# Seven half-block products for the second MLP matrix of a one-core hybrid decoder block, with weight sums added by GpSimd's transfers

## The chip, the cores and the metric

The kernel runs on one core of a Trainium2 chip. The metric is device time in microseconds (us), the median of three runs. TensorE (PE) multiplies, VectorE (DVE) and ScalarE (ACT) do elementwise work, GpSimd (POOL) does little here, and SyncE (SP) issues nearly all transfers. In the profile "PEld" is TensorE's loading of the stationary operand.

## The reference

One layer on a sequence of 512 tokens with 1024 channels: an RMS norm, a token mixer of three branches (mLSTM, GLA, gated DeltaNet), a residual sum, and an MLP with a last norm. What the change mainly touches is the MLP:

```python
u = rmsnorm(x, g_norm_mlp[l])                       # x: (1, 512, 1024)
x = x + jnp.square(jax.nn.relu(u @ w_mlp_in[l])) @ w_mlp_out[l]   # 1024 -> 4096 -> 1024
return rmsnorm(x, g_final)
```

## The kernel before, in words

All large products are made of three float32r matmuls (`mm3`): each operand is split into a rounded part "h" and the rest "l", and l·h, h·l and h·h are added in PSUM. Splitting an operand takes a copy to the rounded type (on ScalarE or VectorE, `either`) and a subtraction on VectorE. Weights come as 512 KB transfers of 128 partitions with 1024 columns into a pool "raw" of three buffers, and are split into pools "wh" and "wl" of three buffers each (`load_w`). `load_w1` does the same for 512 columns in general slots; there are 44 slots of 128x512.

No instruction is placed by hand. `write_block` records all operations in a graph; `Graph.schedule` puts the matmul groups in the order that `plan` names and places every other operation by a list scheduler with fixed costs per operation and due times. `emit` then writes the instructions in that order, so each engine's queue is a fixed sequence and an instruction that waits holds up all behind it. The constant `EVAC` sets how long after its matmuls a PSUM evacuation is due; a transfer is planned at 190e3 bytes per us.

**The first step** ("mv"): for each of eight blocks of 128 channels, SP loads a block of the transposed x (`xk`) and of a weight (`mv0r`, ...). ScalarE scales x by the norm's gain, which lies in `pr`; GpSimd's queue loads `pr`. TensorE makes 96 matmuls into four PSUM banks. Ten warming products of ones come first. For the norm, `gen_u` squares each block (ScalarE), adds the squares (VectorE), and TensorE sums them over the partitions (`token_sums`).

**Before the MLP**, `gen_x2` does the same sum for the second norm, and transposes the residual x2 to token-major tiles. The norm's factor is only needed per token, because relu squared is homogeneous: `r2c` scales the result of the second MLP matrix.

**The MLP** has eight groups of 512 hidden channels. `mlp_in(g)` makes four chunks of 128 channels (24 matmuls of 512 columns each), then relu, square and split into `ah`, `al`. `mlp_out(g)` multiplies with 512 rows of the second matrix: 2 halves of the columns x 4 token tiles x 4 blocks of rows x 3 = 96 matmuls, and VectorE adds each of the eight results, scaled by `r2c`, to x2. The order is mi0, mi1, mo0, mi2, mo1, ... mo7. In the last group each x2 tile is squared after its sum (`square_of`), and `finish` computes the norm's factor and writes a token tile out; the last tile's last half is done in two pieces of 256 columns.

PSUM has eight banks: class "g" (four) holds matmul groups, class "m" (four) the transposes and small products.

The lines that the steps name: `plan`, `gen_u`, `token_sums`, `load_w1`, `gen_x2`, `mlp_in`, `mlp_out`, `square_of`, `finish`, and in the graph `due`, `run` and `record`. All engine work is issued from line 525.

Of the kernel before, what the change touches and what calls it, by code (L numbers as in the profile page):

```python
# [23 lines left out]
NWARM = 10  # L24
# [22 lines left out]
EVAC = 5.0  # L47
# [62 lines left out]
class Op:  # L110
    __slots__ = ("i", "eng", "calls", "cost", "lat", "preds", "succs", "tiles", "main", "fset", "kind", "start", "fin", "lst", "npred", "ready", "new", "tag", "nbytes", "evac", "alts")


class Graph:
    def __init__(self, nc):
        self.nc = nc
        self.ops = []
        self.main_key = None
        self.open = None
        self.shadow = __import__("concourse.bacc", fromlist=["Bacc"]).Bacc("TRN2", target_bir_lowering=False, num_devices=1)  # L120
        self.ntile = 0
# [34 lines left out]
    def record(self, eng, method, a, k):  # L156
# [18 lines left out]
        self.gate = []  # L175
# [99 lines left out]
    def due(self, pin, end):  # L275
# [45 lines left out]
    def run(self, mains, caps, horizon, verbose=False):  # L321
# [66 lines left out]
        while done < total:  # L388
# [147 lines left out]
def plan():  # L536

    seq = """mv mo dk0 mq1 sc mk0 dq1 dq0 mk1 mq0 dk1 gt01 dv0 gt00 dv1 gt02 lq0 gt03 gt20 up00 up02 lk0 lq1 lv lk1 up03 dz up01
    gt22 gt13 up20 gt12 gt21 up21 lr gt23 up22 up23 gt10 up10 up12 gt11 up11 up13 wo mi0""".split()
    for g in range(1, 8):  # L540
        seq += [f"mi{g}", f"mo{g - 1}"]
# [22 lines left out]
def write_block(nc, xT, w_cm, w_tm, w_sc, w_up, w_out, w_mi, w_mo, w_lr, prm, cst, g_fin, out):  # L564
# [58 lines left out]
    nc.gpsimd.dma_start(pr, prm)  # L623
    nc.gpsimd.dma_start(cs[:, :C_LV], cst[:, :C_LV])
# [13 lines left out]
    def token_sums(pss, sums):  # L638
        for t in range(4):
            mm(pss[:, t:t + 1], sums[:, blk(t)], ones)  # L640

    pss = mps("pss")
    rc = one("rc", [P, 4])


    for i in range(NWARM):
        mm(pss[:, P:2 * P], onem, onem)

    def gen_u():
# [8 lines left out]
        nc.vector.tensor_scalar(v, pss[:, :4], 1.0 / D, EPS, op0=ALU.mult, op1=ALU.add)  # L658
# [29 lines left out]
    def load_w1(src, name):  # L688
# [4 lines left out]
        nc.either.copy(h_, r)  # L693
# [72 lines left out]
    pmv = [gps(f"mvp{t}") for t in range(4)]  # L766
    for k in range(8):
# [9 lines left out]
        wh, wl = load_w1(w_tm[G_MV, k // 2, :, k % 2], f"mv{k}")  # L777
        for t in range(4):
            mm3(pmv[t], h_[:, blk(t)], l_[:, blk(t)], wh, wl, k == 0, k == 7)
# [11 lines left out]
    nc.scalar.dma_start(cs[:, C_LV:], cst[:, C_LV:])  # L791
# [14 lines left out]
    eall = one("em", [P, 4, 4, 2, P])  # L806
# [527 lines left out]
    def lv_evac(t, ps):  # L1334
        lv[t] = slot(f"lv{t}")
# [22 lines left out]
    pss2 = mps("pss2")  # L1358
    r2c = one("r2c", [P, 4])

    def gen_x2():
        acc = slot("x2acc")
        for d in range(8):
            sq = tmp(f"x2sq{d}") if d else acc
            nc.scalar.activation(sq, x2T[d], AF.Square)
            if d:
                nc.vector.tensor_add(acc, acc, sq)
            if d == 7:
                token_sums(pss2, acc)
# [30 lines left out]
    gf = [None, None]  # L1400

    def mlp_in(g):
        hs_ = []
        stage[0] = f"mi{g}"
        for i in range(4):
            wh, wl = load_w(w_mi[g * 4 + i], f"mi{g}{i}")
# [5 lines left out]
            a_h = slot("ah", F32R)  # L1412
            a_l = slot("al", F32R)
            nc.scalar.activation(a_h, rl, AF.Square)
            nc.vector.tensor_mul(rl, rl, rl)
            nc.vector.tensor_sub(a_l, rl, a_h.bitcast(F32))
            hs_.append((a_h, a_l))
        return hs_

    def mlp_out(g, hs_):  # L1420
        last = g == NG - 1
        stage[0] = f"mo{g}"
        wts = []
        for hf in range(2):
            w_ = []
            for i in range(2):
                if last and hf:
                    w_ += [load_w1(w_mo[g, hf, i, :, kk], f"mo{g}{hf}{i}{kk}") for kk in range(2)]
                else:
                    wh, wl = load_w(w_mo[g, hf, i], f"mo{g}{hf}{i}")  # L1430
                    w_ += [(wh[:, kk], wl[:, kk]) for kk in range(2)]
            wts.append(w_)
        if last:

            for hf, t, c0, n in [(hf, t, 0, 512) for hf in range(2) for t in range(3)] + [(0, 3, 0, 512), (1, 3, 0, 256), (1, 3, 256, 256)]:
                cl = slice(c0, c0 + n)
                ps = gps(f"mop{g}{t}{hf}{c0}")[:, :n]
                for k in range(4):
                    mm3(ps, hs_[k][0][:, blk(t)], hs_[k][1][:, blk(t)], wts[hf][k][0][:, cl], wts[hf][k][1][:, cl], k == 0, k == 3)
                o = x2[t][hf][:, cl]  # L1440
                nc.vector.scalar_tensor_tensor(o, ps, r2c[:, t:t + 1], o, op0=ALU.mult, op1=ALU.add)
                square_of(t, o)
                if hf and c0 + n == 512:
                    finish(t)
            return
        for hf in range(2):
            for t in range(4):
                ps = gps(f"mop{g}{t}{hf}")
                for k in range(4):
                    mm3(ps, hs_[k][0][:, blk(t)], hs_[k][1][:, blk(t)], wts[hf][k][0], wts[hf][k][1], k == 0, k == 3)  # L1450
                nc.vector.scalar_tensor_tensor(x2[t][hf], ps, r2c[:, t:t + 1], x2[t][hf], op0=ALU.mult, op1=ALU.add)
# [4 lines left out]
    def square_of(t, o):  # L1456
# [3 lines left out]
        if nsq[t] == 1:  # L1460
            nc.vector.tensor_mul(o, o, gf[0])

    def finish(t):

        nc.vector.tensor_mul(x2[t][1], x2[t][1], gf[1])
        f = fss[:, 3 * t:3 * t + 3]
        v, s, y, h = (small(f"f{n}", 1) for n in "vsyh")
        nc.vector.tensor_scalar(v, f[:, 0:1], f[:, 1:2], D * EPS, op0=ALU.add, op1=ALU.add)
        if nsq[t] == 3:
            nc.vector.tensor_add(v, v, f[:, 2:3])  # L1470
        nc.scalar.activation(s, v, AF.Sqrt)
        nc.vector.reciprocal(y, s)

        nc.vector.tensor_scalar(h, y, y, v, op0=ALU.mult, op1=ALU.mult)
        nc.vector.tensor_scalar(h, h, -0.5, 1.5, op0=ALU.mult, op1=ALU.add)
        for hf in range(2):
            nc.vector.tensor_scalar(x2[t][hf], x2[t][hf], y, h, op0=ALU.mult, op1=ALU.mult)
            (nc.scalar if hf else nc.sync).dma_start(out[blk(t), blk(hf, 512)], x2[t][hf])

    prev = mlp_in(0)  # L1480
    for g in range(1, NG):
        cur = mlp_in(g)
        if g == NG - 1:
            gf = [slot(f"gf{hf}") for hf in range(2)]
            for hf in range(2):
                nc.sync.dma_start(gf[hf], g_fin[blk(hf, 512)].partition_broadcast(P))
                nc.vector.tensor_scalar_mul(gf[hf], gf[hf], float(D) ** 0.5)
# [28 lines left out]
def _layout(inp):  # L1516
# [18 lines left out]
    for r in (4, 36, 68):  # L1535
# [14 lines left out]
             w_lr=w_lr, prm=p, cst=_consts(), g_fin=f('g_final'))  # L1550
# [19 lines left out]
```

## Time and profile before

| | |
|---|---|
| median of 3 runs | 976.89 us (976.88 to 976.90) |
| profiled execution | 976.91 us, its span 975.1 us |
| mean granted TensorE clock | 0.996 |
| PE / PEld / DVE / ACT / POOL busy | 99% / 82% / 60% / 42% / 1% of the span |
| moved by transfers | 94.64 MB, mean 97 GB/s |

The span runs from the first to the last instruction; the execution's own time is 1.8 us longer. Busy times are shares of the span; an engine with idle time costs nothing unless the engine that sets the end waits for it.

### The profile page before, as it was taken

Reading aid. Unit: us, or ns where it says so; the run is one execution under the profiler, and the core shown is the slowest. Engines: PE = TensorE matmul, PEld = TensorE weight load, DVE = VectorE, ACT = ScalarE, POOL = GpSimd, SP = SyncE. Lnnn points to the kernel's source line nnn. Section 1 sums busy time; section 2 is a strip of 40 time slices with the busy share of each in tenths; the row PEclk is TensorE's granted clock in tenths of the full one; section 3 lists DMA queues with packets and bytes.
Section 4 is the critical chain, followed back from the end, with each engine's and each line's share of the span. In section 5 each row is a group of like instructions: output and inputs, shape, how many; then the busy total and the mean of one; then the engine's idle time right before and its main releaser. Section 6 shows DMA issues by size and latency. Waiting matters only on the chain.

```text
span 975.1 us, 12773 instructions
## 1 busy us (share of the span) xinstructions
PE 964.2 (99%) x4992; PEld 804.0 (82%) x4992; DVE 580.9 (60%) x1065; ACT 408.5 (42%) x764; POOL 5.4 (1%) x20
## 2 busy tenths in 40 slices
PE   8999999999999999999999999999999999999996
PEld 7888888888888888888888888888888888888885
DVE  6667867778525765777647665444454445544446
ACT  6454466533523664544244434442423233232313
POOL 0000000000000000000000000000000000000000
PEclk9999999999999999999999999999999999999998
DMA  7222532222411222212224222222323224322302
GB/s 269 87 87 87 170 113 95 57 87 88 123 58 66 75 98 87 88 66 76 75 89 142 96 90 94 86 98 87 108 87 109 88 84 153 128 87 87 108 22 87
DMA packets 37028, 94.64 MB, mean 97 GB/s; under 512 B 7804, under 2 KB 11900, under 8 KB 36968
## 3 DMA queue, kind: packets, MB, share of 16 engines
q1 hardware_dynamic: 36152, 92.51, 29.5%
q10 hardware_dynamic: 720, 1.08, 0.3%
q8 instruction: 39, 0.64, 0.3%
q0 software_dynamic: 96, 0.24, 0.1%
q14 instruction: 21, 0.17, 0.1%
HBM read 91.17 MB, written 2.65 MB: 96 GB/s over the span
## 4 chain that ended last, share of the span: by engine, by line
PE 98%; DVE 0%; DMA 0%; ACT 0%; issue 0%; DVEq 0%; POOLq 0%
PE mop L525 20%; PE mip L525 18%; PE upp L525 7%; PE wop L525 4%; PE mvp L525 2%; PE lrp L525 2%; PE dzp L525 2%; PE lvp L525 2%; PE ll L525 2%; PE gt22p L525 1%; PE gt13p L525 1%; PE gt20p L525 1%; PE gt12p L525 1%; PE gt21p L525 1%; PE dq0p L525 1%; PE dv0p L525 1%
## 5 line engine op out<-in xcount | busy, mean ns | idle before, releaser
L525 DVE SCALAR_TENSOR_TENSOR x<-mop,r2c,x 128x512 f32<-128x512 f32 (+1 forms) x65 | 48.1, 741 | 54.0 <-PE mop L525 53.9
L525 DVE TENSOR_TENSOR lw<-lbs 128x260 f32<-128x260 f32 (+12 forms) x52 | 21.0, 448 | 7.9 <-PE ll L525 7.8
L525 DVE SCALAR_TENSOR_TENSOR sg<-sg,upp 128x512 f32<-128x512 f32 x24 | 16.4, 685 | 15.5 <-PE upp L525 15.4
L525 ACT ACTIVATE lw<-lw 128x512 f32<-128x512 f32 x28 | 17.4, 630 | 14.1 <-DVE lw L525 13.8
L525 DVE TENSOR_TENSOR al<-rl,ah 128x512 fp32r<-128x512 f32 x32 | 22.0, 689 | 0.8
L525 DVE TENSOR_TENSOR rl<-rl 128x512 f32<-128x512 f32 x32 | 22.1, 692 | 0.0
L525 PEld LDWEIGHTS ll<-lwq,lw 128*17 128x17 f32 (+3 forms) x320 | 17.5, 131 | 4.3 <-issue 1.4
L525 ACT ACTIVATE ah<-rl 128x512 fp32r<-128x512 f32 x32 | 20.3, 634 | 1.0
L525 ACT ACTIVATE rl<-mip 128x512 f32<-128x512 f32 x32 | 18.9, 591 | 0.0
L525 ACT ACT_TABLE_LOAD x14 | 18.0, 1283 | 1.4 <-PEq L1558 1.2
L525 PE MATMUL ll<-lwq,lw 128*17 128x16 f32 (+3 forms) x320 | 17.9, 214 | 0.0
L525 DVE TENSOR_TENSOR x2T<-xr,wop 128x512 f32<-128x512 f32 x8 | 5.5, 686 | 13.3 <-PE wop L525 13.3
L525 DVE TENSOR_TENSOR lw<-lw,lks 128x260 f32<-128x260 f32 (+6 forms) x28 | 13.1, 498 | 0.0
L525 ACT COPY lAT<-ll 17x64 f32<-17x64 f32 (+3 forms) x32 | 7.2, 231 | 11.4 <-PE ll L525 11.0
L525 DVE COPY_PREDICATED lAT<-cs,ll 128x256 f32<-128x256 uint8 x16 | 9.3, 578 | 4.0 <-PE ll L525 4.0
L525 ACT ACTIVATE fsq<-x 128x512 f32<-128x512 f32 (+1 forms) x9 | 5.3, 585 | 14.1 <-DVE x L525 14.1
L525 DVE TENSOR_TENSOR me<-me,mqk 128x512 f32<-128x512 f32 (+3 forms) x16 | 7.5, 485 | 6.2 <-PE mqk L525 5.9
L525 DVE TENSOR_TENSOR sg<-sg,sg 128x512 f32<-128x512 f32 x16 | 10.8, 688 | 0.2
L525 ACT ACTIVATE cvs<-cv 128x512 f32<-128x512 f32 x12 | 7.5, 628 | 7.4 <-DVE cv L525 7.4
L525 PEld LDWEIGHTS mn<-mv,me 128*128 128x128 f32 x80 | 10.1, 191 | 0.5
L525 ACT ACTIVATE yh<-sg 128x512 fp32r<-128x512 f32 x8 | 5.1, 632 | 13.0 <-DVE sg L525 13.0
L525 PE MATMUL mqk<-mqs,mks 128*128 128x512 f32 (+3 forms) x32 | 10.4, 432 | 0.0
(1584 smaller groups left out, 3178.5 us busy)
## 6 DMA issues: line engine op xcount, KB each, us to landing
xk<-in_xT_dram SPq DMA_DIRECT2D x8, 256.0 KB, 5.6
em<-scr_rows SPq DMA_DIRECT2D x16, 128.0 KB, 4.6
xr<-in_xT_dram SPq DMA_DIRECT2D x8, 256.0 KB, 5.1
nm<-scr_rows SPq DMA_DIRECT2D x4, 256.0 KB, 3.7
out_dram<-x ACTq DMA_DIRECT2D x4, 256.0 KB, 2.1
out_dram<-x SPq DMA_DIRECT2D x4, 256.0 KB, 2.4
mo00r<-in_w_tm_dram SPq DMA_DIRECT2D x1, 512.0 KB, 6.0
mo01r<-in_w_tm_dram SPq DMA_DIRECT2D x1, 512.0 KB
```

What stands on the lines that cost most here:

```text
L525: getattr(getattr(nc, eng), method)(*[f(x) for x in a], **{n: f(x) for n, x in k.items()})
```

## The change

For groups 0 to 6 the second matrix's block (512 tokens x 512 hidden) x (512 hidden x 1024 columns) is taken as 2x2 halves and computed with seven products of halves in place of eight. The sums of weight halves are made in place in four quarter buffers (`bq`, in the memory of `eall`, free by then): SP loads a half, GpSimd issues a transfer that adds another half from HBM onto it (`plus`), five such per group. Sums of activations are made by VectorE from unsplit squares. Products 1 and 6 stay in PSUM ("m" banks) over all groups; 5 and 7 are summed in slots; 2, 3 and 4 go to x2 as before; `join` combines them once, in group 6. Groups' products and chunks are interleaved. Group 7 stays as eight products, with the token loop outermost. The first step's first block runs in three passes over the four tiles; `pr` is issued by ScalarE's queue and `cst` by SP later; x comes a second time, token-major (`x_tm`, 2 MB), to be squared and summed on ScalarE, and the second norm's squares are summed from the transposed tiles. Last factors are computed in a shorter chain, and the last tile is scaled on two engines. `lv` uses the memory of `mv`.

```diff
-NWARM = 10
+NWARM = 9
-EVAC = 5.0
+EVAC = 1.0
...
+    def follow(self, view):
+        self.soft = [o for o, w, *_ in view.t.acc if w]
...
-                l = min([l] + [pin[p] + p.cost + EVAC for p in o.preds if p in pin])
+                l = min(l, max((pin[p] + p.cost for p in o.preds if p in pin), default=1e9) + EVAC)
...
-                dma_free = max(dma_free, T + 0.5) + o.nbytes / 190e3
+                dma_free = max(dma_free, T + 0.5) + o.nbytes / 330e3
...
-        seq += [f"mi{g}", f"mo{g - 1}"]
+        seq += [x if x[0] == "p" else f"mi{g}{x[1]}" for x in ("c0 p1 p7 c1 p5 p6 c2 p4 p3 c3 p2" if g == 7 else "c0 p1 p7 c1 p3 p5 c2 p2 c3 p6 p4").replace("p", f"p{g - 1}").split()]
...
-    nc.gpsimd.dma_start(pr, prm)
-    nc.gpsimd.dma_start(cs[:, :C_LV], cst[:, :C_LV])
+    nc.scalar.dma_start(pr, prm)
...
     def gen_u():
-        acc = slot("xacc")
-        for k in range(8):
-            sq = tmp(f"xsq{k}") if k else acc
-            nc.scalar.activation(sq, xk[k], AF.Square)
-            if k:
-                nc.vector.tensor_add(acc, acc, sq)
-        token_sums(pss, acc)
+        ss = small("ss", 4)
+        for t in range(4):
+            b = eall.rearrange("p h c a t -> p (h c a t)")[:, blk(t, D)]
+            nc.follow(vh[4 + t // 2])
+            nc.sync.dma_start(b, x_tm[t])
+            nc.scalar.activation(b, b, AF.Square, accum_out=ss[:, t:t + 1])
...
+        if k == 0:
+            for i, (a, b) in enumerate(((h_, wh), (l_, wh), (h_, wl))):
+                for t in range(4):
+                    with nc.group(stage[0]):
+                        nc.tensor.matmul(pmv[t], a[:, blk(t)], b, start=i == 0, stop=False)
+            continue
+        if k == 5:
+            nc.follow(x_)
+            nc.sync.dma_start(cs, cst)
...
     def gen_x2():
...
+                    nc.scalar.activation(tmp("x2sq"), ps, AF.Square, accum_out=ss2[:, 4 * hf + t:4 * hf + t + 1])
...
     def mlp_in(g):
...
+            for th in range(2):
+                nc.scalar.activation(a[i // 2][th][:, blk(i % 2, 256)], rl[:, blk(th, 256)], AF.Square)
...
+    def mlp_out(g, a):
+        (a11, a21), (a12, a22) = a
+        x_, y_, b21, b22 = bq
...
+        load(x_, 0, 0)
+        load(y_, 1, 0)
+        plus(y_, 1, 1)
+        load(b22, 1, 1)
+        load(b21, 0, 1)
...
+        def product(n, x, y, nm):
+            xh_, xl_ = split_a(x, f"a{nm}")
+            yh_, yl_ = split_b(y, f"b{g}{nm}")
...
+            for t in range(2):
+                ps = bank[t] if bank else gps(f"pp{g}{n}{t}")
+                for k in range(2):
+                    c = slice(k * 256 + t * P, k * 256 + t * P + P)
+                    mm3(ps, xh_[:, c], xl_[:, c], yh_[:, k], yl_[:, k], k == 0 and (g == 0 or n not in (1, 6)), k == 1 and (tail and n in (1, 6) or not keepon))
...
+        def p_1():
+            product(1, a11, x_, "11")
+            plus(x_, 1, 0)
...
+        def p_5():
+            keep_sum(p5, 5, product(5, s1, x_, "S1"))
+            plus(x_, 1, 1)
+        def p_7():
+            keep_sum(p7, 7, product(7, a21, y_, "S3"))
+            plus(y_, 0, 0)
+            plus(y_, 0, 1)
...
+        nc.vector.tensor_sub(s1, a22, a21)
+        nc.vector.tensor_add(s2, s1, a11)
+        nc.vector.tensor_sub(a21, a11, a21)
+        nc.vector.tensor_sub(s4, a12, s2)
...
     def finish(t):
...
+        nc.scalar.activation(s, l, AF.Sqrt, bias=e)
+        nc.vector.tensor_add(v, l, e)
+        nc.vector.reciprocal(y, s)
+        nc.vector.tensor_scalar(s, y, v, s, op0=ALU.mult, op1=ALU.add)
+        nc.vector.reciprocal(y, s)
...
+        nc.vector.scalar_tensor_tensor(b[:, 256:], b[:, 256:], y, gf[1][:, 256:], op0=ALU.mult, op1=ALU.mult)
+        nc.vector.tensor_scalar_mul(b[:, :256], b[:, :256], y)
+        nc.sync.dma_start(out[blk(t), blk(1, 512)], b)
+        nc.scalar.mul(a, a, y)
+        nc.scalar.dma_start(out[blk(t), blk(0, 512)], a)
```

`split_a` and `split_b` are the copy and subtraction for 512 and 1024 columns. `join` has sixteen VectorE instructions of 512 columns (eight sums and eight scaled additions to x2).

## Rows read from the trace of the kernel before

**Rows 1.** The page's busy times of the engines, share of the span, instructions.
```profile
PE 964.2 (99%) x4992; PEld 804.0 (82%) x4992; DVE 580.9 (60%) x1065; ACT 408.5 (42%) x764; POOL 5.4 (1%) x20
```

**Rows 2.** The chain in order of time: start us, us, what.
```profile
662.21 21.76 PE mop L525 x96
...
923.33 43.68 PE mop L525 x204
```

**Rows 3.** Stretches: length, busy us (instructions) per engine, clock, DMA share, GB/s.
```profile
2.00:18.00 16.00, 14.27 (x59) 11.71 (x58) 12.23 (x21) 13.81 (x27) 0.66 (x5) 0.89 1.01 368
662.20:705.70 43.50, 43.50 (x194) 36.02 (x193) 20.49 (x24) 12.94 (x16) 0.00 (x0) 1.00 0.32 97
...
923.30:975.10 51.80, 43.70 (x205) 36.48 (x203) 28.93 (x56) 13.53 (x29) 0.00 (x0) 0.95 0.14 51
```

**Rows 4.** The timeline: VectorE and ScalarE work before and in the MLP.
```profile
599.66 0.69 DVE L525 CAST wo7h<-wo7r 128x1024 fp32r<-128x1024 f32 x1 [3.66 <-PE wop L525]
...
662.25 1.05 ACT L525 CAST mo010h<-mo010r 128x1024 fp32r<-128x1024 f32 x1 [3.23 <-PE mip L525]
663.20 0.59 ACT L525 ACTIVATE rl<-mip 128x512 f32<-128x512 f32 x1
...
663.34 1.23 DVE L525 TENSOR_TENSOR mo010l<-mo010r,mo010h 128x1024 fp32r<-128x1024 f32 x1 [2.87 <-ACT mo010h L525]
...
665.10 0.74 DVE L525 SCALAR_TENSOR_TENSOR x<-mop,r2c,x 128x512 f32<-128x512 f32 x1
665.76 0.68 DVE L525 TENSOR_TENSOR al<-rl,ah 128x512 fp32r<-128x512 f32 x1
```

**Rows 5.** The timeline of the first 7 us.
```profile
0.73 0.41 ACTq L525 DMA_DIRECT2D cs<-in_cst_dram  x1
...
1.05 3.98 PE L525 MATMUL pss<-onem 128*128 128x128 f32 x20 [1.05 <-DVE onem L525]
...
1.25 0.67 POOL L525 DMA_DIRECT2D pr<-in_prm_dram  x1 [0.80 <-POOLq L1558]
...
4.65 0.20 ACT L525 ACTIVATE scl<-pr 128x1 f32<-128x1 f32 x1 [2.19 <-DMA pr<-in_prm_dram]
4.76 0.70 ACT L525 ACTIVATE vh<-xk,pr 128x512 fp32r<-128x512 f32 x1
...
5.89 0.60 ACT L525 CAST mv0h<-mv0r 128x512 fp32r<-128x512 f32 x1
...
6.54 0.51 PE L525 MATMUL mvp<-mv0h,vl 128*128 128x512 f32 x1 [1.51 <-ACT mv0h L525]
```

**Rows 6.** Stretches of the start, columns as in Rows 3.
```profile
7.60:7.80 0.20, 0.20 (x2) 0.18 (x1) 0.20 (x1) 0.20 (x2) 0.00 (x0) 0.50 0.87 338
...
11.00:11.20 0.20, 0.20 (x2) 0.17 (x1) 0.20 (x1) 0.20 (x1) 0.00 (x0) 0.99 1.09 410
```

**Rows 7.** The timeline: the second step's first matmul, and the second norm's sums.
```profile
31.51 0.39 PE L525 MATMUL mop<-mo00h,vl 128*128 128x512 f32 x1
...
622.39 0.95 PE L525 MATMUL pss<-ones,x2acc 128*128 128x1 f32 x8
```

**Rows 8.** Transfers: issuer, KB each, median us from issue to landing.
```profile
mo010r<-in_w_mo_dram SPq DMA_DIRECT2D x1, 512.0 KB, 3.5
...
cs<-in_cst_dram POOLq DMA_DIRECT2D x1, 192.5 KB, 5.0
...
pr<-in_prm_dram POOLq DMA_DIRECT2D x1, 41.0 KB, 3.4
```

**Rows 9.** The tile xk (eight transfers of 256 KB): issue to landing.
```profile
DMA to landing us min/median/max: 2.8/5.6/6.2
```

**Rows 10.** The timeline of the end.
```profile
967.04 0.48 DVE L525 SCALAR_TENSOR_TENSOR x<-mop,r2c,x 128x256 f32<-128x256 f32 x1 [0.25 <-PE mop L525]
...
968.35 0.20 ACT L525 ACTIVATE fs<-fv 128x1 f32<-128x1 f32 x1 [0.28 <-DVE fv L525]
...
971.53 0.33 SPq L525 DMA_DIRECT2D out_dram<-x  x1
```

More of the change, by code (lines that the diff above doesn't have):

```diff
@@ L110 @@
 class Op:
-    __slots__ = ("i", "eng", "calls", "cost", "lat", "preds", "succs", "tiles", "main", "fset", "kind", "start", "fin", "lst", "npred", "ready", "new", "tag", "nbytes", "evac", "alts")
+    __slots__ = ("i", "eng", "calls", "cost", "lat", "preds", "succs", "tiles", "main", "fset", "kind", "start", "fin", "lst", "npred", "ready", "new", "tag", "nbytes", "evac", "alts", "soft")
 class Graph:
@@ L342, in run @@
             o.npred = len(o.preds)
+            for p in o.soft:
+                if p not in o.preds:
+                    waiting.setdefault(p, []).append(o)
+                    o.npred += 1
             if any(t.cls == "m" for t in o.new):
@@ L636, in write_block, with gen_u @@
     nc.vector.memset(onem, 1.0)
-    def token_sums(pss, sums):
-        for t in range(4):
[L640 to L649, printed above, removed]
-        acc = slot("xacc")
-        for k in range(8):
-            sq = tmp(f"xsq{k}") if k else acc
-            nc.scalar.activation(sq, xk[k], AF.Square)
-            if k:
-                nc.vector.tensor_add(acc, acc, sq)
-        token_sums(pss, acc)
+    eall = one("em", [P, 4, 4, 2, P])
+    rc = one("rc", [P, 4])
+    pmv = [gps(f"mvp{t}") for t in range(4)]
+    for i in range(NWARM):
+        with nc.group("warm"):
+            mm(pmv[3][:, :P], onem, onem)
+    def gen_u():
+        ss = small("ss", 4)
+        for t in range(4):
+            b = eall.rearrange("p h c a t -> p (h c a t)")[:, blk(t, D)]
+            nc.follow(vh[4 + t // 2])
+            nc.sync.dma_start(b, x_tm[t])
+            nc.scalar.activation(b, b, AF.Square, accum_out=ss[:, t:t + 1])
         v = small("v4", 4)
-        nc.vector.tensor_scalar(v, pss[:, :4], 1.0 / D, EPS, op0=ALU.mult, op1=ALU.add)
+        nc.vector.tensor_scalar(v, ss, 1.0 / D, EPS, op0=ALU.mult, op1=ALU.add)
         rsqrt(rc, v, 4)
@@ L692, in load_w1 @@
         h_, l_ = slot(name + "h", F32R), slot(name + "l", F32R)
-        nc.either.copy(h_, r)
+        if eng:
+            nc.vector.tensor_copy(h_, r)
+        else:
+            nc.either.copy(h_, r)
         nc.vector.tensor_sub(l_, r, h_.bitcast(F32))
@@ L764, in smo_evac @@
         nc.scalar.activation(smo[t], ps, AF.Sigmoid, scale=rc[:, t:t + 1])
-    pmv = [gps(f"mvp{t}") for t in range(4)]
     for k in range(8):
@@ L1357, in write_block @@
     x2 = [[None, None] for _ in range(4)]
-    pss2 = mps("pss2")
+    ss2 = one("ss2", [P, 8])
+    r2n = one("r2n", [P, 4])
     r2c = one("r2c", [P, 4])
     def gen_x2():
-        acc = slot("x2acc")
         for d in range(8):
[L1364 to L1369, printed above, removed]
             if d % 4 == 3:
@@ L1400, in write_block @@
     gf = [None, None]
+    bw = eall.rearrange("p h c a t -> p (h c a t)")
+    bq = [bw[:, blk(i, 1024)].rearrange("p (k n) -> p k n", k=2) for i in range(4)]
+    p1, p6 = [mps(f"P1{t}") for t in range(2)], [mps(f"P6{t}") for t in range(2)]
+    p5, p7, us = [None, None], [None, None], [None, None]
     def mlp_in(g):
-        hs_ = []
-        stage[0] = f"mi{g}"
+        a = [[slot(f"A{kh}{th}") for th in range(2)] for kh in range(2)]
         for i in range(4):
+            stage[0] = f"mi{g}{i}"
             wh, wl = load_w(w_mi[g * 4 + i], f"mi{g}{i}")
@@ new lines, in join, with add @@
+    def join():
+        def add(t, hf, v, r):
+            nc.vector.scalar_tensor_tensor(x2[t][hf], v, r[:, t:t + 1], x2[t][hf], op0=ALU.mult, op1=ALU.add)
+        for t in range(2):
+            v = slot(f"v{t}")
+            nc.vector.tensor_sub(v, p6[t], us[t])
+            add(t, 0, us[t], r2c)
+            nc.vector.tensor_sub(us[t], v, p5[t])
+            add(t, 1, us[t], r2c)
+            nc.vector.tensor_sub(p7[t], p7[t], v)
+            add(2 + t, 0, p7[t], r2c)
+            nc.vector.tensor_add(p5[t], p5[t], p7[t])
+            add(2 + t, 1, p5[t], r2n)
@@ L1422, in mlp_out, with mlp_last @@
+    def mlp_last(a):
+        g = NG - 1
         stage[0] = f"mo{g}"
+        hs_ = [split_a(a[kh][th], f"z{kh}{th}") for kh in range(2) for th in range(2)]
         wts = []
@@ L1426, in mlp_out @@
             for i in range(2):
[L1427 to L1431, printed above, removed]
-            wts.append(w_)
[L1433 to L1451, printed above, removed]
+                w_ += [load_w1(w_mo[g, hf, i, :, kk], f"mo{g}{hf}{i}{kk}") for kk in range(2)]
+            wts.append(w_)
@@ new lines, in mlp_last @@
+        for hf, t, c0, n in [(hf, t, 0, 512) for t in range(3) for hf in range(2)] + [(0, 3, 0, 512), (1, 3, 0, 256), (1, 3, 256, 256)]:
+            cl = slice(c0, c0 + n)
+            ps = [p1, p6][hf][t] if t < 2 else gps(f"mop{g}{t}{hf}{c0}")[:, :n]
+            for k in range(4):
+                ah_, al_ = hs_[2 * (k // 2) + t // 2]
+                c = slice(k % 2 * 256 + t % 2 * P, k % 2 * 256 + t % 2 * P + P)
+                mm3(ps, ah_[:, c], al_[:, c], wts[hf][k][0][:, cl], wts[hf][k][1][:, cl], k == 0 and t > 1, k == 3)
+            o = x2[t][hf][:, cl]
+            nc.vector.scalar_tensor_tensor(o, ps, r2c[:, t:t + 1], o, op0=ALU.mult, op1=ALU.add)
+            square_of(t, o)
+            if t == 3 and c0 == 0:
+                nc.vector.tensor_mul(o, o, gf[hf][:, :n])
+            if hf and c0 + n == 512:
+                finish(t)
@@ L1482, in write_block @@
         cur = mlp_in(g)
[L1483 to L1487, printed above, removed]
         mlp_out(g - 1, prev)
         prev = cur
-    mlp_out(NG - 1, prev)
-_INS = ['xT', 'w_cm', 'w_tm', 'w_sc', 'w_up', 'w_out', 'w_mi', 'w_mo', 'w_lr', 'prm', 'cst', 'g_fin']
+    gf = [slot(f"gf{hf}") for hf in range(2)]
+    for hf in range(2):
+        nc.sync.dma_start(gf[hf], g_fin[blk(hf, 512)].partition_broadcast(P))
+        nc.vector.tensor_scalar_mul(gf[hf], gf[hf], 2.0 * float(D) ** 0.5)
+    mlp_last(prev)
+_INS = ['xT', 'w_cm', 'w_tm', 'w_sc', 'w_up', 'w_out', 'w_mi', 'w_mo', 'w_lr', 'prm', 'cst', 'g_fin', 'x_tm']
 def _consts():
```

114 lines of the change are left out of this document (78 added, 36 removed).

## The prediction

> **What bounds the kernel now.** I read the busy times first: TensorE is busy 99% of the span, with weight loading (82%), VectorE (60%) and ScalarE (42%) under it [rows 1]. Then the chain of waits in order of time: in the MLP it is TensorE alone, 21.76 us for each 96 matmuls, without a break until the last group's 43.68 us [rows 2]. So a matmul of 128x512 costs 21.76 / 96 = 0.2267 us, and one that is removed is worth just that while everything else keeps out of the way. The stretches show how much room there is: in one round of 192 matmuls VectorE works 20.49 of 43.5 us, ScalarE 12.94, the transfer engines 0.32 [rows 3]. The timeline of the first 7 us [rows 5] and of the end [rows 10] show the only places where TensorE stands idle: 5.03 to 6.54 us, and after 967.0 us.
>
> **The seven products.** A group goes from 96 matmuls to 7 products x 2 token tiles x 2 blocks of rows x 3 = 84, in seven groups: 7 x 12 = 84 matmuls fewer, x 0.2267 = **19.0 us**. The widths stay at 512 columns and the stationary loads at one per matmul, so the rate should hold. A round becomes 4 x 24 + 84 = 180 matmuls, 40.8 us.
>
> What has to hide under these 40.8 us, with durations from [rows 4], and 0.60 us for a 512-column copy from [rows 5]. VectorE: four chunk splits and seven of weights, 11 x 1.23 = 13.5; seven activation splits and four sums, 11 x 0.68 = 7.5; ten evacuations, 10 x 0.74 = 7.4; 28.4 us in all. ScalarE: 11 copies of 1024 x 1.05, 7 copies of 512 x 0.60, 4 relus x 0.59 and 8 half squares at no more than 0.60: 23 us. Both fit (70% and 56%). Their cost on the path is 0, hidden under TensorE; without the cover VectorE would set the pace only if it needed 12 us more per round. The "g" banks also fit: by the written order every bank that a group of matmuls takes was filled at least one chunk (5.44 us) or two products (5.44 us) before, save one step of 4.1 us, and an evacuation takes 0.74.
>
> In group 6 `join` adds 16 x 0.74 = 11.8 us and group 7's splits 12 x 0.68 = 8.2, while products 2 and 3 no longer need four evacuations (3.0): 45.4 against 40.8 us. The eight additions to x2 in `join` (5.9 us) can wait until the last stretch, where VectorE was idle 22.9 of 51.8 us [rows 3]. Between 0 and 45.4 - 40.8 = 4.6 us; I take 0.5, near the rows, which show no wait of TensorE in the MLP.
>
> **The adding transfers.** The trace of before has none, so I bound one's time L from issue to landing. Below: a plain 512 KB load in the same stage, 3.5 us; GpSimd's own queue landed 192.5 KB in 5.0 and 41 KB in 3.4 us [rows 8]. Above: the slowest 256 KB load of the start, 6.2 us [rows 9], when the transfer engines were full (share 1.01, [rows 3]), twice for twice the bytes: 12.4. I take 6 us: the MLP's share is 0.32 at 97 GB/s, and five additions per round make it (8 + 5) x 0.524 MB / 40.8 us = 167 GB/s, a share near 0.55, so these engines are not full, but each byte is also read from SBUF.
>
> What waits: the buffer `y_` goes through a load, an addition, product 7's split, two additions one after the other, product 4's split, and round again: 3.5 + 3L + 2 x (1.05 + 1.23) = 8.1 + 3L. That fits into 40.8 us while L is under **10.9 us**. `x_` needs 3.5 + 2L + 3 x 2.28 = 10.3 + 2L, under 15. With L = 6 the y ring takes 26 us, so 0. A split that meets a late transfer holds its engine's queue, and behind it stand the relu and the next splits; but with three wh/wl buffers a split is asked for two matmul groups (5.4 us or more) ahead of its use. SP's queue: loads of quarters wait for splits, and chunk loads stand behind them; three raw buffers give these a chunk or two of lead. GpSimd issues five in a round at 0.67 us [rows 5] with nothing else to do. All 0.
>
> **The norms.** The second norm's sums leave TensorE: eight instructions, 0.95 us in the row [rows 7]; the modelled end of the last one overlaps the next matmul, so I take 0.8 us. ScalarE squares the transposed tiles in place of the untransposed, and VectorE loses additions; `r2c` is first used a round later. Off the path.
>
> **The first step.** `pr` was issued by GpSimd at 1.25 and ScalarE began at 4.65, when it had landed; then came vh (0.70), another square, and the copy of mv0r, and TensorE started at 6.54 [rows 5]. ScalarE's queue could issue at 0.73 [rows 5]; with 3.4 us to landing [rows 8] and vh, the first matmul can start at 0.73 + 3.4 + 0.70 + 0.05 = 4.9, since mv0h now is copied by VectorE beside it and the other halves come in later passes. The nine warming products last to 1.05 + 0.9 x 3.98 = 4.6, so the gap shrinks from 1.5 to 0.3 us. Before, the granted clock was 0.50 (the 1.2 GHz level) at 7.6 to 7.8 and back to 0.99 at 11.0 to 11.2 [rows 6], after that gap; with the short gap I expect none of it. Then 96 x 0.2267 = 21.8 us, and without the first norm's sums the next step starts at 26.7; I allow 0.5 us for waits on VectorE, which now makes copy and both differences of the first block in series. Before it started at 31.51 [rows 7]: **4.3 us**. Ends: 4.8 (no wait), and 0.9 (the sums alone, start as before). The 2 MB of x_tm takes 2.1 / 0.368 = 5.7 us of full transfer engines [rows 3]; the next step's weights then land some 6 us later, well before 26 us, as the engines ran full only until about 18. SP has five more issues, at 0.33 to 0.45 us; GpSimd has two fewer.
>
> **The end.** From the last sum (967.04) to the square root 1.31 us, to the last store's issue (971.53) another 3.2 [rows 10]. The new chain after the root: root 0.20, three one-column steps at about 0.2, one scaling of at most 0.74, with the two halves on two engines: issue near 968.3 + 0.2 + 0.6 + 0.7 = 969.8: **1.7 us** less. Ends 0 and 2.3 (a scaling of 256 columns last). `EVAC`, 330e3, `lv` in mv's memory and the rest of the planner change order off the path: 0, covered by TensorE's unbroken chain [rows 2].
>
> **Sum.** 19.0 + 0.8 + 4.3 + 1.7 - 0.5 = 25.3. The profiled execution took 976.91 us (span 975.1 and 1.8 around it), 0.02 over the median 976.89: 976.9 - 25.3 = **951.6 us**.
>
> **Rivals.**
> (a) Hidden as above: 951.6, own range 949 to 957.
> (b) Only the matmuls count: TensorE again waits at the start and the end is as long as before: 976.9 - 19.0 - 0.8 - 0.9 + 0.5 = 956.7. For it: the start hangs on three transfers; against: `pr` was plainly the last to come.
> (c) The adding transfers come late but not past break-even. Either L lies between 10.9 and 12, costing up to 3L + 8.1 - 40.8 = 3.3 us in each of seven rounds, or TensorE meets a held ScalarE or VectorE queue for 1 to 3 us per round: 958.6 to 974.9. A mechanism of its own: GpSimd's issue held up by VectorE's copies, 0.69 us for 1024 columns [rows 4]; if all 35 issues were put off by one and that showed, 35 x 0.69 = 24 us would come back, 975.7. Against it: the only such copies that the rows show are few, as ScalarE takes nearly all, and y has 14 us to spare at L = 6. The Trainium skill ("SBUF — State Buffer", section "SBUF: two separate sides") says that a transfer issued from GpSimd stands still while VectorE runs a two-port copy, since the descriptors cannot be written. No run so far shows it; the trace of after would.
> (d) Slower: additions at L above 12.1. The y ring then takes over 8.1 + 36.3 = 44.4 us per round, 3.6 more than 40.8, and 7 x 3.6 = 25.3 eats the gain. At the bound, L = 12.4, the ring takes 45.3 and the time is 951.6 + 7 x 4.5 = 983. For it: two operands and 128 rows on a queue that the trace hardly shows; against: the transfer engines have half their time free.
> That the change does not do what it says: the number of TensorE instructions tells (4992 - 84 - 16 - 2 = 4890).
>
> **Numbers.** (a) 0.72, (b) 0.10, (c) 0.13, (d) 0.05. The range 948.5 to 960 holds (a), (b) and the foot of (c), so a little over 8 in 10; its low end is the best of every term (19.0 + 0.8 + 4.8 + 2.3 = 26.9, so 950) and 1.5 us for what I missed. A measurement tells about 0.2% (2 us) from no change. Faster: (a), (b) and nearly all of (c), 0.93; the same: the top of (c), 0.02; slower: (d), 0.05.
>
> **What would show it.** Right: 4890 instructions; rounds of 40.8 us in the chain with no wait in them; first matmul of mv near 4.9 and no stretch at 0.50 clock after it; second step from about 27; 35 transfers from GpSimd landing within 10.9 us; the last store about 2.8 us after the last sum. Wrong: TensorE waiting for splits in each round at product 7 or 4, with the releaser a copy that itself waits for `y_`; rounds of equal and longer length; the first step's clock falling all the same.

## The result, and the profile after

The changed kernel takes 954.77 us (median of 4 runs, 953.17 to 955.07) against 976.88 of the kernel before: a ratio of 0.9774, 95% interval 0.9757 to 0.9791. The profiled execution took 955.07 us, its span 953.3, so 21.84 us less than the profiled execution of before (976.91). The forecast was 951.6; the 3.5 us between it and the profiled execution are what the experiments had to find. The 36 runs of the kernel before that stand beside the sets here come in two lengths, 975.2 to 975.5 and 976.5 to 977.4 us, and the profiled one is of the longer.

The page's busy times, then pieces of the chain in order of time (P: the banks of products 1 and 6, in group 6 of 2 and 3 too; pp: those of the other products; mip: a chunk; em: a quarter buffer), then the stretches of one full round and of group 6 (columns as in [rows 3]), answering to [rows 1], [rows 2] and [rows 3]:

```profile
PE 943.1 (99%) x4890; PEld 786.0 (82%) x4890; DVE 617.8 (65%) x1119; ACT 457.0 (48%) x876; POOL 34.6 (4%) x53
```

```profile
682.08 2.72 PE P L533 x12
684.80 2.72 PE pp L533 x12
687.52 5.44 PE mip L533 x24
...
891.44 7.38 DMA em<-in_w_mo_dram
901.28 2.79 PE P L533 x11
904.06 5.46 PE mip L533 x24
913.27 2.97 PE P L533 x12
```

```profile
682.08:722.88 40.80, 40.80 (x181) 33.78 (x181) 26.33 (x34) 19.97 (x30) 4.31 (x5) 1.00 0.68 168
...
886.08:926.88 40.80, 38.66 (x168) 31.17 (x168) 31.83 (x44) 18.46 (x32) 1.75 (x2) 1.00 0.21 38
```

The count of TensorE instructions is the one forecast, and six rounds take 40.80 us each with TensorE busy for all of it: a product is 12 x 0.2267 = 2.72 us, a chunk 5.44. VectorE works 26.3 us of a round, ScalarE 20. Only in the round of group 6 are 168 matmuls done where 181 fit: 13 x 0.2267 = **2.95 us lost**. The waits of TensorE after its first matmul are all in that round:

```profile
PE P L533 <- DVE aS4l L533: 1.0, 1, 1.0
PE P L533 <- DVE b6S2l L533: 0.8, 1, 0.8
PE P L533 <- ACT b6S2h L533: 0.3, 1, 0.3
```

(`aS4l` is the rest part of the split activations of product 3; `b6S2h` and `b6S2l` are the two parts of `x_` as product 6 of group 6 uses it; `b6S1h` and `b6S1l` those of product 5.)

The timeline of group 6 on ScalarE, GpSimd and VectorE shows where they begin (start, length, engine, work, in brackets the idle time before it and what ended it):

```profile
888.84 1.05 ACT L533 CAST b6S1h<-em 128x1024 fp32r<-128x1024 f32 x1 [0.70 <-PE P L533]
889.92 1.22 DVE L533 TENSOR_TENSOR b6S1l<-em,b6S1h 128x1024 fp32r<-128x1024 f32 x1 [0.28 <-ACT b6S1h L533]
890.83 1.75 POOL L533 DMA_DIRECT2D em<-in_w_mo_dram  x2 [6.07 <-DMA em<-in_w_mo_dram]
...
898.91 1.05 ACT L533 CAST b6S2h<-em 128x1024 fp32r<-128x1024 f32 x1 [7.40 <-DMA em<-in_w_mo_dram]
899.87 0.59 ACT L533 ACTIVATE rl<-mip 128x512 f32<-128x512 f32 x1
```

Product 5's split of `x_` ends at 891.14; only then may the third part be added. Its issue is the second of the two in the GpSimd row, at 891.44, 0.61 us behind one for `y_`, and it lands 7.4 us later, at 898.8. Product 6, the next one in the written order, needs that sum. Its copy holds ScalarE's queue for 7.40 us, with a relu and the next splits behind it.

The transfers (issuer, KB each, median us to landing), answering to [rows 8]:

```profile
em<-in_w_mo_dram POOLq DMA_DIRECT2D x35, 512.0 KB, 6.4
em<-in_w_mo_dram SPq DMA_DIRECT2D x28, 512.0 KB, 3.4
```

An adding transfer lands after 6.4 us, a plain one of the same size after 3.4. The start and the second step's first matmul, for [rows 5] and [rows 7], and two stretches for [rows 6]:

```profile
0.73 0.41 ACTq L533 DMA_DIRECT2D pr<-in_prm_dram  x1
...
3.72 0.20 ACT L533 ACTIVATE scl<-pr 128x1 f32<-128x1 f32 x1 [1.27 <-DMA pr<-in_prm_dram]
...
5.02 2.01 PE L533 MATMUL mvp<-mv0h,vh 128*128 128x512 f32 x4
...
27.78 0.39 PE L533 MATMUL mop<-mo00h,vl 128*128 128x512 f32 x1
```

```profile
7.00:9.00 2.00, 2.00 (x11) 1.60 (x10) 1.83 (x3) 1.52 (x4) 0.00 (x0) 1.00 1.00 376
9.00:11.00 2.00, 2.00 (x10) 1.65 (x9) 1.61 (x4) 1.94 (x4) 0.00 (x0) 1.00 1.06 405
```

ScalarE's wait for the gain ends 3.0 us after its issue, the first matmul starts at 5.02 in place of 6.54, the clock stays at 1.00 where it was 0.50 before, and the second step begins 31.51 - 27.78 = 3.73 us earlier. The end, for [rows 10]:

```profile
946.50 0.48 DVE L533 SCALAR_TENSOR_TENSOR x<-mop,r2c,x 128x256 f32<-128x256 f32 x1
...
947.35 0.74 DVE L533 SCALAR_TENSOR_TENSOR x<-x,fy,gf 128x512 f32<-128x512 f32 x1
947.55 0.29 ACT L533 ACTIVATE fs<-fss,fe 128x1 f32<-128x1 f32 x1
948.02 0.15 DVE L533 TENSOR_TENSOR fv<-fss,fe 128x1 f32<-128x1 f32 x1
...
949.53 0.39 ACTq L533 DMA_DIRECT2D out_dram<-x  x1
```

From the last sum to the span's end it takes 953.3 - 946.50 = 6.80 us; before, 975.1 - 967.04 = 8.06.

### The profile page after: what moved, and what is told of

Same layout as the page of the kernel before. It is cut to its first block, busy times and chain, and to the rows that moved or that the text cites. A ratio compares the mean times of both kernels' runs of the same rounds, so it can differ in the third digit from the quotient of the medians.

```text
span 953.3 us, 12850 instructions
## 1 busy us (share of the span) xinstructions
PE 943.1 (99%) x4890; PEld 786.0 (82%) x4890; DVE 617.8 (65%) x1119; ACT 457.0 (48%) x876; POOL 34.6 (4%) x53
## 4 chain that ended last, share of the span: by engine, by line
PE 93%; issue 3%; DMA 1%; DVE 1%; ACT 0%; POOL 0%; DVEq 0%; ACTq 0%; POOLq 0%
PE mip L533 15%; PE pp L533 7%; PE upp L533 7%; PE P L533 5%; PE wop L533 5%; PE mop L533 3%; PE mvp L533 3%; PE lrp L533 2%; PE dzp L533 2%; PE lvp L533 2%; PE ll L533 2%; DMA em<-in_w_mo_dram 1%; PE gt21p L533 1%; PE gt13p L533 1%; PE gt20p L533 1%
## 5 line engine op out<-in xcount | busy, mean ns | idle before, releaser
L533 POOL DMA_DIRECT2D em<-in_w_mo_dram x35 | 30.4, 875 | 491.2 <-DVE b011l L533 244.1
L533 DVE SCALAR_TENSOR_TENSOR x<-pp,r2c,x 128x512 f32<-128x512 f32 x38 | 27.1, 746 | 2.4 <-PE pp L533 2.4
L533 ACT ACTIVATE A<-rl 128x256 f32<-128x256 f32 x64 | 23.6, 410 | 0.6
L533 DVE TENSOR_TENSOR P<-P,pp 128x512 f32<-128x512 f32 x24 | 16.0, 682 | 3.2 <-PE pp L533 3.2
L533 ACT COPY lAT<-ll 17x64 f32<-17x64 f32 (+3 forms) x32 | 7.1, 231 | 10.9 <-PE ll L533 10.4
L533 PE MATMUL mqk<-mqs,mks 128*128 128x512 f32 (+3 forms) x32 | 10.7, 432 | 0.0
L533 PE MATMUL mn<-mv,me 128*128 128x129 f32 x80 | 10.2, 275 | 0.0
```

The costliest lines, as they stand in the source:

```text
L533: getattr(getattr(nc, eng), method)(*[f(x) for x in a], **{n: f(x) for n, x in k.items()})
```

## The experiments

Two theories for the lost 2.95 us stood against each other. A: the late third part of `x_`, since product 6 follows product 5 directly. B: VectorE is overloaded in group 6 by `join` and the last group's splits (31.83 us busy in that round). Each time below is a median; the kernel before ran beside each set, and the ratio is to it.

**1. A chunk between products 5 and 6, and with it product 3 behind the last chunk.**

```diff
-"c0 p1 p7 c1 p5 p6 c2 p4 p3 c3 p2" if g == 7
+"c0 p1 p7 c1 p5 c2 p6 p4 c3 p3 p2" if g == 7
```

> The kernel after, with one edit: in the last seven-product group the chunk c2 stands between product 5 and product 6 (order c0 p1 p7 c1 p5 c2 p6 p4 c3 p3 p2). Theory A (the late third part of x_): product 6 follows product 5 on the same buffer, its addition lands 7.4 us after product 5's split, and the wait holds ScalarE and then VectorE; with 5.44 us more between them the 2.1 us of TensorE's waits in group 6 go: 954.8 - 2.1 = 952.7 us. Theory B (VectorE overloaded by join and the splits of the last group): the waits on b6S2 go (1.1 us), the wait on aS4l stays or grows, since join now starts 5.4 us later: 953.7 to 955.5 us.

Measured: 952.43 us, ratio 0.9760 [0.9747, 0.9773]. After its first matmul TensorE has no wait left, and the stretch of group 6 is full:

```profile
886.10:926.90 40.80, 40.80 (x182) 33.63 (x181) 32.60 (x47) 20.46 (x35) 1.73 (x2) 1.00 0.20 37
```

VectorE is as busy as before (32.60 us), so its load alone made no wait. For the waits on b6S2 this is A. For the one on aS4l this run decides nothing: the new order also puts chunk c3 ahead of product 3, which gives its split 5.44 us more. Experiment 3 keeps the order.

**2. A chunk and a product between them.** Order `c0 p1 p7 c1 p5 c2 p2 p6 c3 p4 p3`, and the products are recorded in that order too.

> The kernel after, with one edit: order c0 p1 p7 c1 p5 c2 p2 p6 c3 p4 p3 in the last seven-product group, so that a chunk and a product (8.2 us) stand between products 5 and 6. Theory A: no wait of TensorE is left on a split of b6S2, and none on aS4l: 952.7 us. Theory B: join now begins 8.2 us later and runs into the last group's splits, so TensorE waits on VectorE for aS4l or the z splits: 954 us or more.

Measured: 955.29 us, 0.9788 [0.9774, 0.9801]. The waits on b6S2 are gone, but one stays, and 177 matmuls fit into the stretch:

```profile
PE P L533 <- DVE aS4l L533: 0.9, 1, 0.9
```

So B is no fiction: `join` starts 6.4 us later than in the kernel after (909.92 in place of 903.47), product 3 follows product 4 directly again, and its split stands on VectorE behind `join`'s sums, and the last norm's scalings pile up too: from the last sum to the span's end it takes 953.3 - 944.36 = 8.94 us, against 7.43 in experiment 1. B limits how the loss may be mended; whether A names what was lost is for the next experiment.

**3. One adding transfer left out; all left out.**

```diff
         def p_5():
             keep_sum(p5, 5, product(5, s1, x_, "S1"))
-            plus(x_, 1, 1)
+            if not tail:
+                plus(x_, 1, 1)
```

For all 35 the body of `plus` is `pass`.

> The kernel after without one of its 35 adding transfers, the third part of x_ in group 6 (product 6 of that group is then made with an incomplete sum of weights); the order of the products stays. Theory A: the chain from product 5's split to product 6's split is the cause, so all of the 2.1 us go: 952.7 us, and no ScalarE wait of 7.4 us. Theory B: VectorE's work is the same, so the wait on aS4l stays: 953.7 us or more.

> The kernel after without any of the 35 adding transfers (products 1, 5, 6, 7 and 4 are made with unsummed weights). Theory A: in groups 0 to 5 the transfers were wholly hidden, so rounds stay at 40.80 us and only group 6's 2.1 us go: 952.7 us. Rival C (the additions' traffic slows the stage as a whole, by reads of SBUF or full transfer engines): the rounds get shorter than 40.80 us, and the time falls under 951.5 us.

Measured: 952.09 us, 0.9754 [0.9741, 0.9768], without the one; 951.60 us, 0.9751 [0.9737, 0.9764], without all 35. Neither leaves a wait of TensorE after its first matmul. The stretch of group 6 without the one, and a round without any:

```profile
886.10:926.90 40.80, 40.80 (x182) 33.78 (x181) 33.26 (x46) 19.68 (x33) 0.86 (x1) 1.00 0.15 26
...
682.08:722.88 40.80, 40.80 (x182) 33.78 (x181) 26.32 (x33) 20.01 (x31) 0.00 (x0) 1.00 0.32 104
```

The order of the products is that of the kernel after, VectorE is busier (33.26 us against 31.83), and the wait on aS4l is gone with those on b6S2. So A names what was lost. Between the profiled executions, 955.07 - 951.67 = 3.4 us is what all the additions cost, and a single one of them costs 955.07 - 952.12 = 2.95. Rounds without any are 40.80 us, as with five, at a share of the transfer engines of 0.32 in place of 0.68: the traffic itself is hidden, and C (the rival in the second expectation) falls.

**4. The second matrix alone as before.** `mlp_in` and `mlp_out` of the kernel before for groups 0 to 6, with their order; start, norms and end of the kernel after.

> The kernel after with the second MLP matrix of groups 0 to 6 as before (eight products, no additions, chunk groups and product groups in turn); new start, norms and end stay. The sum: 84 matmuls come back, 19.0 us, and the waits of group 6, 2.9 us, go: 954.8 + 19.0 - 2.9 = 970.9 us. Rival: the waits of the last groups come from the last eight-product group and not from the seven products: 973.8 us. Rival: the transfers cost something in every round, so that the seven products gain less than the count: under 969.5 us.

Measured: 970.83 us, 0.9945 [0.9929, 0.9962], no wait of TensorE in the MLP. The products are worth 970.83 - 954.77 = 16.06 us net, which is 19.0 less the 2.95 lost.

**5. The first step as before, in three tries.** Gain by GpSimd's queue, no passes, first norm's squares summed by TensorE.

> The kernel after with its first step undone (ten warming products, the gain from GpSimd's queue, the first block not in passes, the first norm's squares added by VectorE and summed by TensorE). If the start stands alone, as in the sum, the second step begins at 31.5 us in place of 27.8 and nothing later gives it back: 954.8 + 3.7 = 958.5 us (957.7 to 959.5). Rival: only the first norm's sums count, since the transfers of the start set the pace of the first step anyway: 954.8 + 0.9 = 955.7 us.

Measured: 963.41 us, 0.9873 [0.9856, 0.9889]: nothing that was expected. The planner, with the new due times, put all eight blocks of x ahead of the weights, TensorE waited 5.8 us for `mv0h`, and the clock fell in that gap and stayed low behind it (0.50 in both stretches):

```profile
9.00:11.00 2.00, 0.00 (x0) 0.00 (x0) 1.90 (x4) 2.00 (x5) 0.00 (x0) 0.50 1.05 393
11.00:13.00 2.00, 0.79 (x1) 0.29 (x1) 1.90 (x4) 2.00 (x4) 0.00 (x0) 0.50 1.04 385
```

> The kernel after with its first step undone, as in the earlier run of that kind, but with the due times of the first step's banks as before, so that SP again issues a block of x and its weights in turn (the earlier run loaded all of x first). If the start stands alone, the second step begins at 31.5 us in place of 27.8, with a stretch at clock 0.50 behind the gap: 954.8 + 3.7 = 958.5 us (957.7 to 959.5). Rival: what the start gains is given back later, since the second step then waits for its own transfers or the norm's factor: under 956.5 us.

Measured: 961.24 us, 0.9849 [0.983, 0.9869]. SP's order was that of before, but the warming products had slipped behind the first three matmuls. Neither try undoes the part and nothing else. The third adds to the second:

```diff
+        if k == 0:
+            nc.after(pss)
         for t in range(4):
             mm3(pmv[t], h_[:, blk(t)], l_[:, blk(t)], wh, wl, k == 0, k == 7)
```

> The kernel after with its first step undone, a third time: the warming products are now also held ahead of the first matmul (in the second try the planner put them behind the first three matmuls, where they held TensorE for 3.8 us), and SP's order is that of before. If the start stands alone, the second step begins at 31.5 us in place of 27.8: 954.8 + 3.7 = 958.5 us (957.7 to 959.5). Rival: the rest of the kernel gives it back: under 956.5 us. Rival: the old start costs more than in the kernel before, since its other work is ordered for the new one: above 959.5 us.

Measured: 955.71 us, 0.9791 [0.9778, 0.9804], under every figure but the rival's. The trace says why in two parts: the first two matmuls, a stretch, and the second step's first matmul:

```profile
6.33 0.47 PE L534 MATMUL mvp<-mv0h,vl 128*128 128x512 f32 x1 [1.14 <-DVE vl L534]
6.85 0.50 PE L534 MATMUL mvp<-mv0l,vh 128*128 128x512 f32 x1
...
29.45 0.39 PE L534 MATMUL mop<-mo00h,vl 128*128 128x512 f32 x1
```

```profile
9.00:11.00 2.00, 2.00 (x10) 1.68 (x9) 2.00 (x4) 2.00 (x5) 0.00 (x0) 1.00 1.06 394
```

The gap before the first matmul is 1.14 us here, 1.51 in [rows 5], and this time the clock did not fall. So the old start costs 29.45 - 27.78 = 1.67 us, not 3.73. The MLP's first matmul is still 1.55 us late (613.61 against 612.06). Then group 6's stretch holds 176 matmuls where the kernel after holds 168, and 8 x 0.2267 = 1.8 us come back there. The written order of the products is the same, but the third part of `x_` is issued 2.1 us behind the addition to `y_` in place of 0.61 and lands in 5.6 us in place of 7.4; the waits on b6S2 are gone and only the one on aS4l (0.9 us) is left. So the order costs its 2.95 us only together with a late landing; what the spacing of two issues does to a landing was not tested by itself.

The start's gain is 1.67 us where the clock stays up and some 2 us more where it falls, as it did in the profiled execution of before. Of these 2 us the clock itself takes 1.6: eight matmuls from 7.61 to 11.02 need 3.41 us there, where 8 x 0.2267 = 1.81 would do.

**6. The last norm as before**, on the kernel of experiment 1.

> The kernel with c2 between products 5 and 6 (952.4 us), its last norm undone (factors and scaling as before). From the last sum to the last store's issue before took 4.49 us, in this kernel 3.62: 952.4 + 0.9 = 953.3 us. By the sum's own term of 1.7 us it would be 954.1 us. Rival: the end is set by VectorE's backlog of scalings, which both forms have: 952.4 us.

Measured: 956.87 us, 0.9799 [0.9785, 0.9814]. Its end takes 955.4 - 947.47 = 7.93 us from the last sum, close to before's 8.06, against 7.43 in experiment 1 and 6.80 after. From the last sum to the last issue it takes 4.20 us, where 4.49 was expected. The rest of the time has two parts, both in group 6. The planner's new order brought in a wait of TensorE of 2.2 us for `a22l` from VectorE, from 907.84 to 910.02, and behind it the clock fell:

```profile
912.00:914.00 2.00, 2.00 (x6) 1.51 (x6) 1.07 (x2) 0.00 (x0) 0.00 (x0) 0.50 0.00 0
```

From 911.31 to 914.67 eight matmuls take 3.36 us in place of 1.81, another 1.5 us. So the time is no measure of the end; the rows are. By them the new form of the norm is worth 0.5 us in the kernel of experiment 1, where VectorE's scalings stand ahead of it, and 1.26 between the two profiled executions.

**7. Each adding transfer twice.**

> The kernel after with each of the 35 adding transfers issued twice (sums of weights hold a part twice). By the ring formula the y buffer takes 8.1 + 6 x 6.4 = 46.5 us per round against 40.8, so 5.7 us per round are lost in six rounds or more: 954.8 + 34 to 40 = 989 to 995 us, with TensorE waiting for y_'s splits in every round. Rival: two additions in succession overlap, so that a pair costs little over one (7 us): the ring stays under 40.8 and the time within 2 us of 954.8.

Measured: 1028.87 us, ratio 1.0538 [1.0523, 1.0554]: twice the loss forecast. The transfers (median landing last), the first addition of two rounds on GpSimd, and a stretch over some three and a half rounds:

```profile
em<-in_w_mo_dram POOLq DMA_DIRECT2D x70, 512.0 KB, 6.9
em<-in_w_mo_dram SPq DMA_DIRECT2D x28, 512.0 KB, 4.5
```

```profile
785.50 0.86 POOL L533 DMA_DIRECT2D em<-in_w_mo_dram  x1 [11.13 <-DMA em<-in_w_mo_dram]
...
835.91 0.86 POOL L533 DMA_DIRECT2D em<-in_w_mo_dram  x1 [10.94 <-DMA em<-in_w_mo_dram]
```

```profile
641.28:820.00 178.72, 159.93 (x634) 127.42 (x633) 90.50 (x110) 71.11 (x109) 28.94 (x34) 0.91 0.79 180
```

TensorE waits in every round, and the rival falls. It could not have come true here: the kernel's graph lets a write to a buffer start only when the one before has landed, so this says nothing of whether the chip could overlap two additions. The ring is longer than worked out, since under the load an addition lands in 6.9 us and a load in 4.5, 1.0 more than before: 1.0 + 8.1 + 6 x 6.9 = 50.5 us. The round above takes 835.91 - 785.50 = 50.4; the six from group 0 to group 6 take 47.6 to 56.6, in the mean (944.29 - 632.80) / 6 = 51.9. That is near the formula, but GpSimd's queue, in which the additions to `x_` and `y_` stand behind each other, could set such a round as well; the two were not told apart. By the first chunk's weights of group 7, copied at 939.1 in place of 875.2, six rounds lost 63.9 us, 10.7 each; group 6 lost the rest. While TensorE waits its granted clock falls too, to a mean of 0.91 in this stretch; whether that costs anything beside the ring is open too.

**8. VectorE copies beside GpSimd's issues.**

```diff
-        nc.either.copy(h_, x)
+        nc.vector.tensor_copy(h_, x)
```

in `split_b`, and likewise for the chunks' weights.

> The kernel after with all copies of the MLP's weight splits on VectorE (some 77 copies of 128x1024 at 0.69 us moved from ScalarE; VectorE goes from 26 to 34 of 40.8 us per round). Rule of the Trainium skill (SBUF page, two separate sides): GpSimd's issue stands still while VectorE copies, so issues that fall on a copy take up to 0.86 + 0.69 = 1.55 us and additions land later; the y ring stays under 8.1 + 3 x 7.1 = 29.4 us, so it shows in the rows of the issues and not in the time. Rival: issues keep 0.86 us beside the copies. In either case the time is set by VectorE's queue: 954 to 958 us, above 956 if TensorE meets late splits.

Measured: 956.51 us, 0.9798 [0.9784, 0.9813]; the rounds of groups 0 to 5 stay at 40.80 us with VectorE at 33 us, the loss is in group 6 (waits for aS4l, mi72l and b6S2l). An issue that met a copy, one that met another VectorE instruction:

```profile
839.86 1.29 POOL L533 DMA_DIRECT2D em<-in_w_mo_dram  x1 [3.94 <-DVE b511l L533]
840.37 0.69 DVE L533 CAST b5S3h<-em 128x1024 fp32r<-128x1024 f32 x1
...
649.62 0.86 POOL L533 DMA_DIRECT2D em<-in_w_mo_dram  x1 [4.82 <-DVE b0S1l L533]
649.83 0.69 DVE L533 TENSOR_TENSOR a22l<-A,a22h 128x512 fp32r<-128x512 f32 x1
```

Five issues inside which a whole copy fell took 1.17 to 1.29 us; the others took 0.86 or 0.87 (two without a gap between them 1.75 together), those beside sums and those that overlapped a copy by 0.2 us or less among them. The Trainium skill ("SBUF — State Buffer", section "SBUF: two separate sides") says that a transfer issued from GpSimd stands still while VectorE runs a two-port copy. The trace agrees: the five are 0.31 to 0.43 us longer, less than the copy's 0.69 to 0.80, and each ends 0.07 to 0.10 us after its copy does (the one above at 841.15, the copy at 841.06). So what was left of an issue waited for the end of the copy. The additions did not land later for it (5.5 us in the median). In the kernel after no issue took longer for it, since ScalarE makes nearly all copies.

**9. A version that beats both.** Experiment 1's order, and in the last norm tile 2 taken off VectorE:

```diff
-            if t == 3 and c0 == 0:
-                nc.vector.tensor_mul(o, o, gf[hf][:, :n])
+            if t > 1 and c0 == 0:
+                (nc.vector if t == 3 else nc.gpsimd).tensor_mul(o, o, gf[hf][:, :n])
...
+        if t == 3:
+            nc.after(s)
+            nc.scalar.mul(x2[2][1], x2[2][1], y2[0])
...
+                if t == 2:
+                    nc.gpsimd.tensor_scalar_mul(x2[t][hf], x2[t][hf], y)
...
```

> The kernel with c2 between products 5 and 6, and in the last norm tile 2's halves multiplied by the gain on GpSimd ahead of time, one half scaled on GpSimd and one on ScalarE right behind tile 3's square root, so that VectorE has no scaling of 0.74 us between the last steps of tile 3's factor. If that backlog is what lengthens the end (3.62 us from the last sum to the last issue, where 2.7 would do): 951.5 us. Rival: GpSimd's products take so long, or slow VectorE so far, that the last store waits for them: 952.4 us or more.

Measured: 951.96 us, 0.9752 [0.9737, 0.9766].

```profile
943.81 0.48 DVE L533 SCALAR_TENSOR_TENSOR x<-mop,r2c,x 128x256 f32<-128x256 f32 x1
...
944.86 0.16 DVE L533 TENSOR_TENSOR fv<-fss,fe 128x1 f32<-128x1 f32 x1
...
946.65 0.37 ACTq L533 DMA_DIRECT2D out_dram<-x  x1
```

From last sum to last issue it takes 2.84 us in place of 3.62 in experiment 1 (3.03 in the kernel after), near the 2.7 expected; the medians, 951.96 and 952.43, differ by less than their intervals, so the order of the products is what is shown to gain over the kernel after (the five runs of experiment 1, 952.31 to 952.89, all lie under the four of that kernel), and the end is shown only in the rows.

## Why the prediction was right, and where it was off

By the two profiled executions, term by term:

| term | forecast | measured |
|---|---|---|
| first step | 4.3 | 31.51 - 27.78 = 3.73 |
| second norm's sums | 0.8 | 29.95 - 29.06 = 0.89, from the MLP's first matmul to the end of its fifth chunk (615.78 to 645.73 before, 612.06 to 641.12 after) |
| 84 matmuls | 19.0 | 19.0 |
| group 6 | -0.5 | -2.95 |
| end | 1.7 | 8.06 - 6.80 = 1.26 |
| sum | 25.3 | 21.9, of 21.84 between the executions |

The misses lie nearly all on one side, so the total did not come out by their cancelling.

**Seven products: right.** Count, rate and rounds of 40.80 us are as worked out, with VectorE at 26 of the 28.4 us allowed and ScalarE at 20 of 23; undoing them alone costs 16.06 us, the 19.0 less group 6. (The 19.0 in the table is count times rate; this run is what bears it out.)

**Adding transfers: right on average, wrong at one place.** L was taken as 6 and measured 6.4 in the median and 8.3 at most; rival (d) needed 12.1 and rival (c) 10.9. The share of the transfer engines in a round is 0.68 where 0.55 was worked out, and GpSimd's issue takes 0.86 us where 0.67 was taken; neither cost anything. The step that failed is "a split is asked for two matmul groups ahead of its use" together with the ring of `x_`, 10.3 + 2L against 40.8. A ring over a round says nothing of the distance between two uses inside it. In groups 0 to 5 two chunks and product 2 stand between products 5 and 6; in group 6 none does, and the sum needs 2.28 + 7.4 + 2.28 us there. This is the small end of what rival (c) describes (a wait that holds ScalarE's queue), in one round of seven.

**`join`'s overload: the term of 0.5 was mis-sized, and its cause misnamed.** 2.95 us were lost. Experiment 3 shows that the wait on aS4l, which looks like VectorE's, goes as well when that one transfer is left out, with the order and VectorE's load as they were; experiment 2 shows that VectorE would set a limit of its own.

**The start: mechanism right, size off by 0.6.** First matmul at 5.02 (4.9 forecast), no clock of 0.50 (forecast). From there to the second step 22.76 us pass against 21.8 + 0.5 allowed. Experiment 5 adds that only 1.67 us of the 3.73 are sure; of the other 2.06 the clock's fall behind the gap is 1.6.

**The end: off by 0.4.** The chain of factors is as short as forecast, but a scaling of tile 2 (0.74 us at 947.35) stands on VectorE ahead of `fv`, which starts at 948.02, 0.5 us after ScalarE's sum was read, and the stretch from the last issue to the span's end is 0.2 us longer. Experiment 9 removes the scaling.

**Rival (c)'s mechanism**, the issue held by VectorE's copies, is real at 0.31 to 0.43 us an issue in experiment 8; in the changed kernel it lengthened none.

## What to carry to other kernels

A buffer that is refilled in place has two limits: the ring over a round, and the distance between two uses that follow each other; the second has to be read from the written order, above all in the round that differs from the others. Where a planner places the instructions, undoing one part moves others (in four of the twelve kernels here that hid what the edit was to show): read the waits and the order before putting a difference in time down to the edit.

## What the runs showed of the hardware that was not expected

- An adding transfer of 512 KB lands in 6.4 us in the median, a plain load of the same block in 3.4; in the other kernels with the additions made once the medians are 5.5 to 6.4 and 3.3 to 3.6. With twice as many they are 6.9 and 4.5. In the kernel after, single ones take 5.2 to 8.3 us.
- With a gap of 1.51 us before the first matmul the granted clock went to 0.50 in one execution [rows 6], with one of 1.14 us it stayed at 1.00 in another; in the MLP a wait of 2.2 us was followed by a fall (experiment 6), waits of 1.0 us were not. Each of these two falls cost 1.5 to 1.6 us beside the gap. How often it falls was not measured.
- GpSimd multiplies a tile of 128x512 in 1.64 to 1.85 us (the three of experiment 9); VectorE takes 0.68 to 0.75.
